# A hybrid decoder layer: the residual of the first token blocks added by engines, the third pair's weight parts ahead of spare sums, the last token block stored plainly

## The chip, the cores and the metric

The kernel runs on one core of a Trainium2 chip. Its engines work side by side and each takes its instructions in order: TensorE (PE in the profile, with PEld for its weight loads), VectorE (DVE), ScalarE (ACT), GpSimd (POOL) and SyncE (SP), which issues most transfers. The metric is the device time of one execution in microseconds (us), lower is better.

## The reference

One decoder layer on 1,024 tokens of width 1,024, in float32. What bears on this change is the frame around the two sub-layers, and the gated MLP:

```python
h = rms_norm(x, g_pre_mix[i]) * (1.0 + sc1) + sh1
...
x = x + gt1 * rms_norm(y @ w_out[i], g_post_mix[i])
h = rms_norm(x, g_pre_ffn[i]) * (1.0 + sc2) + sh2
x = x + gt2 * rms_norm(conv_ffn(h, w_up[i], ffn_conv_w[i], w_down[i]), g_post_ffn[i])
```

`conv_ffn` multiplies by `w_up` (1,024 x 5,632), runs a causal convolution of width 3 over tokens, applies `silu(a) * v` and multiplies by `w_down` (2,816 x 1,024). Between `h` and `y` stand a state-space mixer and a gated short convolution.

## The kernel before

Every product is made of three TensorE products: each factor is split into a high part (a cast on ACT) and a low part (a difference on VectorE or GpSimd), and the product of the two low parts is left out. The helper `mm3` (lines 475 to 479) issues them, and `tt` and `stt` (lines 867 and 870) are the two common VectorE operations, so these lines stand for many places; the tile names tell them apart.

**Order.** All work is written as generators ("threads"), and a planner, `Flow`, puts their steps in order before anything runs. A step names an engine and a cost (`D_` VectorE, `A_` ScalarE, `G_` GpSimd, `M_` TensorE, `L_` a transfer), or it waits for an event, for a free buffer of a ring (`get`), or for the landing of the thread's last transfer (`land`). The planner always takes the step that can start first, and among steps that can start within 0.02 us on that engine, the one with the lowest number in `PRIO`. It counts 2.1 us from the end of an issue to the landing. `SITES` says which engines may take an element-wise step; for `x2` that is VectorE alone. On the chip, each engine then runs its list in that order, waiting on semaphores; a step that waits holds all that stand behind it on its engine.

**The stage around the first residual.** The output projection (`t_out`) goes over three token blocks: block 0 of 512 tokens, blocks 1 and 2 of 256 each. A block has four tiles (`dp`), each with two groups of 128 channels. ACT scales a tile out of PSUM into `og` and squares it into `oq` (lines 1604 and 1606); the squares are summed, TensorE and some small steps make the norm of each token (`token_rstd`, lines 491 and 501), and then `t_resid` starts `t_x2` once for each tile: VectorE multiplies `og` by the norm, the input `x` is added, ACT squares the sum into `xr` (line 1713), SP stores it to `x2_dr`, and the squares are summed. `xr` is one of the four tables CL, Tr, Tz and St, left over from the mixer; `t_xr` hands them out, and CL keeps the sum of squares of its block until the second norm has been made. In blocks 0 and 1 the input is added by an accumulating transfer that POOL issues (line 1710), so `xr` is only a place for the squares. In block 2 `t_xr` loads the input into `xr` and VectorE adds it. After the second norm, `t_h2` makes the MLP's input, split into `h2h` and `h2l`.

**The up-projection** works on pairs of channel tiles (22 pairs). Pairs 0 and 1 are plain products (`t_ahead`, `t_first`): their parts on block 0, then those on block 1 and 2. From pair 2 on (`t_up`), a pair is a Strassen-Winograd product: seven products of 512 by 512, with the sums S1 to S4 of quarters of the MLP's input (`t_forms`, `t_forms2`) and sums of quarters of the weights. `t_pair_weights(i)` loads the two weight tiles of a pair, splits the first as it is (part a), makes differences, and splits them as part b, T2 and t; T2 and t lie in tiles named `wf` and `hm`. Pair 2 runs its products in the order 1 6 2 4 5 3 7: product 1 takes part a; 6 takes T2 and S2; 2 part a; 4 and 5 part t (5 with S1); 3 and 7 part b (with S4 and S3). The threads of the sums have the numbers 8.2 to 9.5, all of `t_pair_weights` 13. Behind the products come the convolution's taps on VectorE (`t_gate2`, number 2).

**The end.** The down-projection is another Strassen-Winograd product, seven products P1, P2, P5, P7, P6, P3 and P4 in this order, each over four token blocks of 128 (`tb`). `t_evict` and `t_half` put the eight blocks of the output together in halves of 512 columns, square and scale them; `t_final(b)` makes the norm of block `b`, has ACT scale each half by it (line 2364), and POOL add it to the output in memory by an accumulating transfer (line 2366). The output holds the transposed residual by then: `t_x2t` has put it there. The block made last is 7.

Of the kernel before, what the change touches and what calls it, by code (L numbers as in the profile page):

```python
# [16 lines left out]
ADD, SUB, MUL = ALU.add, ALU.subtract, ALU.mult  # L17

P = 128
# [5 lines left out]
H = 512  # L25
# [36 lines left out]
def _constants():  # L62
# [66 lines left out]
PRIO = {  # L129
    "t_small": 0,  # L130
    "t_loads": 6.0,
    "t_norm0": 7,
    "t_x": 1,
    "t_sh": 9,
    "t_h": 3.5,
    "t_u": 9.5,
    "t_bias": 0.5,
# [177 lines left out]
def hybrid_layer(ctx, tc, xT, w_adaT, w_ada0, w_u, w_bcv, w_out, w_up, w_down, glu_w, vec, ssm, con, out):  # L315
    nc = tc.nc
    outB = out.rearrange("(b p d) -> b p d", p=P, d=D)
    pe, dve, act, pool = nc.tensor, nc.vector, nc.scalar, nc.gpsimd
# [14 lines left out]
    fl = Flow({"k2": NK2, "k4": NK4, "hl": NHL, "raw": NRAW, "big": 3, "sm": 2, "nrm": 2, "s4": 0, "sn": 0, "wf0": 0, "wf1": 0, "hm0": 0, "hm1": 0, "cv": 0, "ca": 0, "gs": 0, "t5": 0, **{t: 1 for t in tables}})  # L333
# [3 lines left out]
    def nm(s):  # L337
        uid[0] += 1
        return f"{s}_{uid[0]}"
# [16 lines left out]
    def table(s, shape):  # L356
        return sp.tile([P] + shape, F32, tag=s, name=nm(s), bufs=1)

    def load(dst, src):
        nc.sync.dma_start(dst, src)  # L360


    def D_(n):
        return ("run", "dve", 0.07 + 1.04e-3 * n)

    def A_(n):
        return ("run", "act", 0.094 + 0.833e-3 * n)
# [7 lines left out]
    def L_(kb):  # L375
        return ("load", "dma", max(0.45, kb * 2.85e-3))

    def T_(site, o, a, b, op, n):

        e = yield ("pick", *({"dve": D_, "pool": G_}[e](n)[1:] for e in SITES[site]))  # L380
        {"dve": dve, "pool": pool}[e].tensor_tensor(o, a, b, op)  # L381
# [37 lines left out]
    def C(name, lo=0, hi=None):  # L419
        a, b = _CC[name]  # L420
        return ct[:, a + lo : (b if hi is None else a + hi)]
# [444 lines left out]
    def tt(o, a, b, op, eng=None):  # L866
        (eng or dve).tensor_tensor(o, a, b, op)  # L867

    def stt(o, a, s, b, op0, op1):
        dve.scalar_tensor_tensor(o, a, s, b, op0, op1)  # L870
# [654 lines left out]
    blocks = ((0, 0, H), (1, 0, H // 2), (1, H // 2, H))  # L1525
# [51 lines left out]
    def add_squares(site, bi, acc, q, i, n):  # L1577

        if i == 0:
            acc.append(q)  # L1580
        elif i == NT - 1 and bi == len(blocks) - 1 and SUM_ON_PE:
            acc.append(q)
        else:
            yield from T_(site, acc[0], acc[0], q, ADD, 2 * n)
# [92 lines left out]
    ev_xr = [[Event() for _ in range(NT)] for _ in blocks]  # L1677

    def t_xr():

        yield ("wait", ev_stat["a"])
        for bi, (hf, lo, hi) in enumerate(blocks):
            n = hi - lo
            for dp in range(NT):
                tag = ("CL", "Tr", "Tz", "St")[dp]
                yield ("get", tag)
                xr = table(tag, [1024])[:, : 2 * n]
                if bi == 2:
                    yield L_(n)
                    load(xr.rearrange("p (a t) -> p a t", a=2), x_of(bi, dp))  # L1690
                ev_xr[bi][dp].tile = xr, tag
                fl.fire(ev_xr[bi][dp], bi == 2)

    def x_of(bi, dp):
        hf, lo, hi = blocks[bi]
        return xT[2 * dp * P : (2 * dp + 2) * P, hf * H + lo : hf * H + hi].rearrange("(a p) t -> p a t", a=2)

    def t_x2(bi, dp, sl, n, og, r1, s2):

        two = "p (a t) -> p a t"  # L1700
        yield D_(2 * n)
        o3 = og.rearrange(two, a=2)
        tt(o3, o3, r1.unsqueeze(1).to_broadcast([P, 2, n]), MUL)
        yield ("wait", ev_xr[bi][dp])
        xr, tag = ev_xr[bi][dp].tile
        if bi == 2:
            yield from T_("x2", og, og, xr, ADD, 2 * n)
        else:
            yield ("load", "pool", 1.0)
            pool.dma_start(o3, x_of(bi, dp), accum_op=ADD)  # L1710
            yield ("land",)
        yield A_(2 * n)
        act.activation(xr, og, AF.Square)
        yield L_(n)
        load(x2_dr[2 * dp * P : (2 * dp + 2) * P, sl].rearrange("(a p) t -> p a t", a=2), o3)
        if dp:
            yield ("wait", s2[2][dp - 1])
        n_acc = len(s2[0])
        yield from add_squares(("sum_x2", "sum_x2", "sum_x2_last")[bi], bi, s2[0], xr, dp, n)
        if len(s2[0]) == n_acc:  # L1720
            fl.put(tag)
        else:
            s2[1].append(tag)
        fl.fire(s2[2][dp])
        if dp == NT - 1:
            fl.fire(ev_x2[bi], True)
# [73 lines left out]
    fl.spawn(t_out(), PRIO["t_out"])  # L1800
    fl.spawn(t_ahead(), PRIO["t_ahead"])
    fl.spawn(t_xr(), PRIO["t_xr"])


# [3 lines left out]
    def ptile(p, tag, shape, dt, bufs=1):  # L1808
        return pools[p].tile([P] + shape, dt, tag=tag, name=nm(tag), bufs=bufs)

    def E_(n, elsewhere=False):

        return ("run", "dve", 0.155 + 1.045e-3 * n)
# [65 lines left out]
    def hl_tile():  # L1879
        return hp.tile([P, 2, 1024], F32R, tag="hl", name=nm("hl"))  # L1880

    def odd_even(what, i):

        return ptile("ab"[i % 2], what, [2, 1024 if what == "hm" else H], F32R)

    def split(t, w, n, site="split_d"):

        yield A_(n)
        act.copy(t[:, 0, :n], w)  # L1889
        yield from TT_(site, t[:, 1, :n], w, t[:, 0, :n].bitcast(F32), SUB, n)  # L1890

    def TT_(site, o, a, b, op, n):
        if SITES[site] == ("dve",):
            yield from dve_tt(o, a, b, op, n)
        else:
            yield from T_(site, o, a, b, op, n)
# [5 lines left out]
    def t_pair_weights(i):  # L1902
        ev = pw[i]
        yield ("wait", pw[i - 1]["loaded"] if i > 2 else wev["up", NFF + 1][2])
        yield ("get", "raw", 2)
        wa, wb = (wp.tile([P, 1024], F32, tag="raw", name=nm("w")) for _ in range(2))
        yield L_(512)
        load(wa, w_up[i])
        yield L_(512)
        load(wb, w_up[NFF + i])  # L1910
        fl.fire(ev["loaded"])
        yield ("land",)
        yield ("wait", pw[i - 1]["t"] if i > 2 else wev["up", NFF + 1][0])
        yield ("get", "hl")
        ev["a"].tile = hl_tile()
        yield from split(ev["a"].tile, wa, 1024, "split_a")
        fl.fire(ev["a"])
        b11, b21, b12, b22 = wa[:, :H], wa[:, H:], wb[:, :H], wb[:, H:]

        yield from TT_("wsum" if i > 2 else "split_d", b11, b12, b11, SUB, H)  # L1920
        yield from TT_("wsum" if i > 2 else "split_d", b12, b22, b12, SUB, H)
        yield ("get", "hl")
        ev["b"].tile = hl_tile()
        yield from split(ev["b"].tile, wb, 1024)
        fl.fire(ev["b"])
        yield from TT_("wsum" if i > 2 else "split_d", b22, b22, b11, SUB, H)
        q = i % 2
        yield ("get", f"wf{q}")
        ev["T2"].tile = odd_even("wf", q)
        yield from split(ev["T2"].tile, b22, H)  # L1930
        fl.fire(ev["T2"])
        yield from TT_("wsum" if i > 2 else "split_d", b21, b21, b22, SUB, H)
        fl.put("raw")
        yield ("get", f"hm{q}")
        ev["t"].tile = odd_even("hm", q)
        yield from split(ev["t"].tile, wa, 1024)
        fl.put("raw")
        fl.fire(ev["t"])
# [108 lines left out]
    def cv(tag):  # L2047
        return ptile("ba"[tag == "ca"], tag, [T], F32, NCA if tag == "ca" else NCV)
# [61 lines left out]
    ev_x2t = Event()  # L2110
# [122 lines left out]
    NTB = NB // 2  # L2233
    LATE = 7
    banks = {}
    ev_prod = {(p, tb): Event() for p, _ in PRODUCTS for tb in range(NTB)}
# [113 lines left out]

    def t_final(b):

        for c in range(2):
            yield ("wait", ev_half[b, c])
        f = fin[:, b, :]
        yield D_(1)
        tt(f[:, 0:1], f[:, 0:1], f[:, 1:2], ADD)
        r = f[:, 1:2]
        yield from rsqrt(r, f[:, 0:1], 1.0 / D, (f[:, 2:3], f[:, 3:4]), EPS, 1, C("eps", 0, 1))
        yield ("wait", ev_x2t)  # L2360
        for c in range(2):
            u, of = half[b, c]
            yield A_(H + 100)
            act.activation(u, u, AF.Copy, scale=r)
            yield ("load", "pool", 1.0)
            pool.dma_start(outB[b, :, c * H : (c + 1) * H], u, accum_op=ADD)  # L2366
            if of:
                fl.spawn(t_put(of), 0)
        yield ("land",)

    def t_put(tag):
        yield ("land",)
        fl.put(tag)
# [20 lines left out]
        for dp in range(2):  # L2394
            fl.spawn(t_forms(s, dp), PRIO["forms"][s])
    for i in range(2, NFF):
        fl.spawn(t_pair_weights(i), PRIO["weights"])
    fl.spawn(t_x2t(), PRIO["t_x2t"])
    fl.spawn(t_all_up(), PRIO["t_ffn"])
    fl.spawn(t_gate2(), PRIO["t_gate2"])  # L2400
# [88 lines left out]
```

## Time and profile before

| What | us |
|---|---|
| Median of 3 runs | 1170.17 |
| Lowest and highest | 1169.62 and 1173.97 |
| The profiled execution | 1169.3 |
| Its span, first to last instruction | 1167.5 |

The profile is of one execution. The page gives each engine's busy time; the view of waits says which instruction waited for which; the view by stretch gives busy time within a part of the span, with the clock that TensorE was granted as a share of full speed; the order of time lists instructions with their start, their length, and in brackets the idle time before them with what ended it. A row such as `og<-og,CL` names the tiles written and read. Times of matmuls overlap, since they are pipelined. The rough order of the span: the mixer up to about 370 us, the output projection with the residual up to about 490 us, the pairs of the up-projection up to about 940 us, and the down-projection up to 1156 us.

### The profile page before, as it was taken

The page shows a single profiled execution, that of the slowest core. Times are in us where ns is not written, and L with a number is a line of the kernel's source. Part 1 is how long each engine was busy: PE and PEld are TensorE (multiplying, and loading weights), DVE is VectorE, ACT ScalarE, POOL GpSimd, SP SyncE. Part 2 cuts the span into 40 slices and gives each one's busy share as a digit, 9 for nine tenths or more (in the row PEclk, how much of TensorE's full clock was granted, in tenths as well). Part 3 has the DMA queues.
Part 4 walks back from the last instruction along what each step waited for, and adds up shares of the span by engine and source line. Part 5 has one row for each costly group of instructions (what it writes and reads, how often), then busy time and mean ns, then how long its engine had stood idle before and what let it go on. Part 6 is the DMA issues. An engine that isn't in the chain of part 4 may idle for free.

```text
span 1167.5 us, 13965 instructions
## 1 busy us (share of the span) xinstructions
PE 1056.0 (90%) x5012; PEld 855.6 (73%) x5012; DVE 877.8 (75%) x1212; ACT 486.7 (42%) x676; POOL 473.6 (41%) x475
## 2 busy tenths in 40 slices
PE   2987999999779956897999999999999999999995
PEld 2765778778446956785788888888888887888884
DVE  6769768897996335898778897889879978554752
ACT  4435322232344423555343333433433456454453
POOL 4799455652594022201444443434444320242013
PEclk9978989999899977799999999999999999999998
DMA  7533312337652274642532332233224498999338
GB/s 278 223 138 128 113 37 77 95 129 246 224 198 84 80 163 125 189 143 75 189 131 96 113 131 83 81 125 120 86 77 134 165 270 262 256 210 296 103 65 123
DMA packets 88533, 171.02 MB, mean 146 GB/s; under 512 B 8720, under 2 KB 34064, under 8 KB 88464
## 3 DMA queue, kind: packets, MB, share of 16 engines
q1 hardware_dynamic: 77648, 151.25, 37.9%
q0 software_dynamic: 10816, 18.88, 10.0%
q8 instruction: 39, 0.64, 0.2%
q14 instruction: 30, 0.25, 0.1%
HBM read 132.64 MB, written 37.46 MB: 146 GB/s over the span
## 4 chain that ended last, share of the span: by engine, by line
PE 44%; POOL 15%; issue 15%; DVE 12%; DMA 9%; ACT 3%; SPq 1%; POOLq 0%; DVEq 0%; ACTq 0%
PE big L475 9%; PE big L477 9%; PE big L479 9%; PE sm L475 5%; PE sm L479 5%; PE sm L477 5%; DMA wd<-in_w_down_dram 3%; POOL pa L381 2%; DMA w<-g_dr 2%; POOL Pt L381 1%; POOL wd L2217 1%; POOL out_dram L2366 1%; POOL pt L894 1%; POOL yl L381 1%; POOL pt L900 1%
## 5 line engine op out<-in xcount | busy, mean ns | idle before, releaser
L381 POOL TENSOR_TENSOR hl<-w,hl 128x1024 fp32r<-128x1024 f32 x34 | 86.8, 2554 | 253.6 <-ACT hl L1889 145.6
L381 POOL TENSOR_TENSOR w<-w,w 128x512 f32<-128x512 f32 x57 | 86.3, 1514 | 83.1 <-DVE hl L867 80.1
L1889 ACT CAST hl<-w 128x1024 fp32r<-128x1024 f32 (+1 forms) x65 | 66.5, 1023 | 49.4 <-issue 20.2
L2217 POOL DMA_DIRECT2D wd<-in_w_down_dram x44 | 38.3, 891 | 113.2 <-PE big L2266 29.4
L475 PE MATMUL big<-yh,hl 128*128 128x256 f32 (+1 forms) x192 | 67.7, 352 | 13.3 <-ACT hl L461 13.1
L867 DVE TENSOR_TENSOR wl<-wd,wh 128x512 fp32r<-128x512 f32 x77 | 51.0, 686 | 36.6 <-ACT wh L2221 36.6
L479 PE MATMUL big<-yh,hl 128*128 128x256 f32 (+1 forms) x192 | 65.9, 343 | 13.0 <-POOL hl L381 11.6
L477 PE MATMUL big<-yl,hl 128*128 128x256 f32 (+1 forms) x192 | 65.9, 343 | 7.6 <-POOL yl L381 7.6
L2221 ACT CAST wh<-wd 128x512 fp32r<-128x512 f32 x77 | 46.8, 620 | 54.8 <-DMA wd<-in_w_down_dram 53.5
L870 DVE SCALAR_TENSOR_TENSOR ca<-big,vec,ca 128x896 f32<-128x896 f32 (+1 forms) x92 | 65.1, 740 | 4.5 <-ACT ca L2055 4.5
L479 PE MATMUL big<-h,hl 128*128 128x512 f32 x192 | 60.8, 399 | 5.2 <-POOL hl L381 5.2
L475 PE MATMUL big<-h,hl 128*128 128x512 f32 x192 | 63.2, 411 | 0.8 <-DVE yb L867 0.4
L867 DVE TENSOR_TENSOR hl<-w,hl 128x1024 fp32r<-128x1024 f32 (+1 forms) x45 | 52.8, 1174 | 14.6 <-ACT hl L1889 14.6
L461 ACT CAST hl<-w 128x1024 fp32r<-128x1024 f32 x43 | 44.8, 1045 | 44.8 <-PE big L479 31.5
L475 PE MATMUL big<-s,hl 128*128 128x512 f32 x160 | 63.2, 395 | 0.0
L477 PE MATMUL big<-s,hl 128*128 128x512 f32 x160 | 63.1, 394 | 0.0
L479 PE MATMUL big<-s,hl 128*128 128x512 f32 x160 | 62.9, 393 | 0.0
L477 PE MATMUL big<-h,hl 128*128 128x512 f32 x192 | 61.3, 399 | 1.3 <-DVE h L725 1.3
L870 DVE SCALAR_TENSOR_TENSOR cv<-big,vec,cv 128x896 f32<-128x896 f32 (+1 forms) x84 | 58.3, 739 | 5.3 <-ACT cv L2055 5.3
L475 PE MATMUL big<-h2h,hl 128*128 128x512 f32 (+1 forms) x160 | 60.4, 378 | 0.0
L479 PE MATMUL big<-h2h,hl 128*128 128x512 f32 (+1 forms) x160 | 59.6, 373 | 0.7 <-DVE hl L381 0.7
L477 PE MATMUL big<-h2l,hl 128*128 128x512 f32 (+1 forms) x160 | 59.6, 373 | 0.0
(359 smaller groups left out, 3178.7 us busy)
## 6 DMA issues: line engine op xcount, KB each, us to landing
w<-in_w_up_dram SPq DMA_DIRECT2D x44, 512.0 KB, 4.0
w<-g_dr SPq DMA_DIRECT2D x35, 512.0 KB, 5.6
g_dr<-cv SPq DMA_DIRECT2D x53, 256.0 KB, 2.3
wd<-in_w_down_dram SPq DMA_DIRECT2D x44, 256.0 KB, 7.4
wd<-in_w_down_dram POOLq DMA_DIRECT2D x44, 256.0 KB, 6.5
w<-in_w_out_dram SPq DMA_DIRECT2D x20, 512.0 KB, 3.3
WBT<-in_w_adaT_dram SPq DMA_DIRECT2D x16, 512.0 KB, 3.7
w<-in_w_bcv_dram SPq DMA_DIRECT2D x13, 512.0 KB, 3.6
```

Source lines behind the costliest of these rows:

```text
L381: {"dve": dve, "pool": pool}[e].tensor_tensor(o, a, b, op)
L461: act.copy(t[:, 0, :], w)
L475: pe.matmul(outs[i], wh, xh[i], start=start, stop=False)
L477: pe.matmul(outs[i], wh, xl[i], start=False, stop=False)
L479: pe.matmul(outs[i], wl, xh[i], start=False, stop=stop)
L867: (eng or dve).tensor_tensor(o, a, b, op)
L870: dve.scalar_tensor_tensor(o, a, s, b, op0, op1)
L894: small_steps.append(lambda e: [lambda: e.tensor_tensor(o, a, b, op)])
L900: return [lambda: e.tensor_scalar(tT, a, s, None, op0), lambda: e.tensor_tensor(o, tT, b, op1)]
L1889: act.copy(t[:, 0, :n], w)
L2217: pool.dma_start(w, block_of(made[1], kk), accum_op=ADD)
L2221: act.copy(hi, w)
```

## The change

There are three parts. In the first, `t_xr` loads the input for all three blocks, and `t_x2` adds it in all three as it did in block 2 alone. The function `x_of` goes. In the second, the thread of pair 2's weights gets the number 8.9. In the third, `t_final` treats blocks 3 and 7 in another way: once P3 of token block 0 is done and the residual stands in the output, it takes a tile of the ring `cv` and loads the 128 rows into it; VectorE multiplies each half by the norm and adds the loaded residual in one operation, and SP stores the half.

```diff
                 xr = table(tag, [1024])[:, : 2 * n]
-                if bi == 2:
-                    yield L_(n)
-                    load(xr.rearrange("p (a t) -> p a t", a=2), x_of(bi, dp))
+                yield L_(n)
+                load(
+                    xr.rearrange("p (a t) -> p a t", a=2),
+                    xT[2 * dp * P : (2 * dp + 2) * P, hf * H + lo : hf * H + hi].rearrange("(a p) t -> p a t", a=2),
+                )
                 ev_xr[bi][dp].tile = xr, tag
-                fl.fire(ev_xr[bi][dp], bi == 2)
+                fl.fire(ev_xr[bi][dp], True)
...
         xr, tag = ev_xr[bi][dp].tile
-        if bi == 2:
-            yield from T_("x2", og, og, xr, ADD, 2 * n)
-        else:
-            yield ("load", "pool", 1.0)
-            pool.dma_start(o3, x_of(bi, dp), accum_op=ADD)
-            yield ("land",)
+        yield from T_("x2", og, og, xr, ADD, 2 * n)
...
     def t_final(b):
 
+        plain = b % NTB == NTB - 1
+        if plain:
+            yield ("wait", ev_prod["P3", 0])
+            yield ("wait", ev_x2t)
+            yield ("get", "cv")
+            x = cv("cv")
+            yield L_(512)
+            load(x, outB[b])
+            yield ("land",)
...
         for c in range(2):
             u, of = half[b, c]
+            if plain:
+                sl = slice(c * H, (c + 1) * H)
+                yield E_(H)
+                stt(x[:, sl], u, r, x[:, sl], MUL, ADD)
+                yield L_(256)
+                load(outB[b, :, sl], x[:, sl])
+                continue
             yield A_(H + 100)
             act.activation(u, u, AF.Copy, scale=r)
             yield ("load", "pool", 1.0)
...
     for i in range(2, NFF):
-        fl.spawn(t_pair_weights(i), PRIO["weights"])
+        fl.spawn(t_pair_weights(i), 8.9 if i == 2 else PRIO["weights"])
```

More of the change, by code (lines that the diff above doesn't have):

```diff
@@ L1687, in t_xr @@
                 xr = table(tag, [1024])[:, : 2 * n]
-                if bi == 2:
-                    yield L_(n)
-                    load(xr.rearrange("p (a t) -> p a t", a=2), x_of(bi, dp))
+                yield L_(n)
[3 more added lines that the diff above has]
+                )
                 ev_xr[bi][dp].tile = xr, tag
-                fl.fire(ev_xr[bi][dp], bi == 2)
-    def x_of(bi, dp):
-        hf, lo, hi = blocks[bi]
-        return xT[2 * dp * P : (2 * dp + 2) * P, hf * H + lo : hf * H + hi].rearrange("(a p) t -> p a t", a=2)
+                fl.fire(ev_xr[bi][dp], True)
     def t_x2(bi, dp, sl, n, og, r1, s2):
```

## The prediction

> **What bounds it now.** I read the page's busy table first, then who TensorE waited for, then busy time by stretch, then the order of time inside the worst stretch.
>
> ```profile
> span 1167.5 us, 13965 instructions
> PE 1056.0 (90%) x5012; PEld 855.6 (73%) x5012; DVE 877.8 (75%) x1212; ACT 486.7 (42%) x676; POOL 473.6 (41%) x475
> ```
>
> TensorE is the busiest engine by far, so what it loses in idle time, or at a low clock, is the time to win. The waits of PE in 410 to 560 us (total, times, longest) are the largest it has after the convolution:
>
> ```profile
> PE big L475 <- ACT hl L461: 13.1, 1, 13.1
> PE big L479 <- POOL hl L381: 11.6, 1, 11.6
> PE sm L475 <- ACT wf L1889: 6.7, 1, 6.7
> ```
>
> Busy time by stretch (length, then PE, PEld, DVE, ACT, POOL, granted clock, DMA share, GB/s):
>
> ```profile
> 410.00:560.00 150.00, 112.86 (x647) 101.00 (x646) 106.12 (x180) 71.48 (x128) 29.61 (x16) 0.82 0.51 144
> 480.00:560.00 80.00, 71.33 (x390) 60.55 (x389) 71.70 (x130) 45.45 (x86) 12.40 (x5) 0.93 0.44 147
> 560.00:600.00 40.00, 39.55 (x183) 32.15 (x183) 29.15 (x33) 16.47 (x20) 17.94 (x12) 1.00 0.45 151
> 431.00:451.00 20.00, 17.19 (x84) 16.72 (x85) 8.28 (x17) 6.95 (x13) 3.51 (x2) 0.59 0.53 143
> 470.00:482.00 12.00, 10.99 (x61) 10.79 (x62) 9.96 (x19) 6.51 (x10) 2.65 (x2) 0.66 0.51 146
> ```
>
> In 410 to 560 PE is idle 150 - 112.86 = 37.1 us, and after each long wait it works at a clock of 0.59 and 0.66: 17.19 x 0.41 + 10.99 x 0.34 = 10.8 us more. From 560 on (39.55 of 40 busy) it is nearly full until the end. So the 150 us around the residual are the place, and they are lost to this:
>
> ```profile
> 428.45 1.06 ACT L1713 ACTIVATE Tz<-og 128x1024 f32<-128x1024 f32 x1 [5.10 <-DMA og<-in_xT_dram]
> 429.42 0.46 ACT L1604 ACTIVATE og<-big,col 128x256 f32<-128x256 f32 x1
> 429.77 1.03 ACT L461 CAST hl<-w 128x1024 fp32r<-128x1024 f32 x1
> ```
>
> The square of the new residual stands on ACT until the accumulating transfer has landed; behind it in ACT's queue stands the cast of the next output weights, and PE stands until that cast is done (the 13.1 us above). The 11.6 us are the same thing one block later. The transfers (their tile's view):
>
> ```profile
> L1710 POOL DMA_DIRECT2D og<-in_xT_dram x8: 1204/1214/1398, 410.0 to 466.4; - x8
> DMA to landing us min/median/max: 4.2/5.3/8.0
> ```
>
> Each transfer is issued only after the square before it, so four latencies stand in a row in each block.
>
> **Edit 1: eight engine adds in place of eight accumulating transfers.** It removes the transfers above and about 8 x 1.21 = 9.7 us of POOL issue. It adds eight VectorE adds; the rows of their shapes, two inputs in SBUF, are (x, then total and mean ns):
>
> ```profile
> L381 DVE TENSOR_TENSOR CL<-CL,Tr 128x1024 f32<-128x1024 f32 x1 | 1.2, 1225 | 8.5 <-ACT Tr L1713 8.5
> L381 DVE TENSOR_TENSOR og<-og,CL 128x512 f32<-128x512 f32 x1 | 0.7, 685 | 0.0
> ```
>
> 4 x 1.225 + 4 x 0.685 = 7.6 us of DVE. The chain of a block gets shorter by far. Now, first multiply to last sum:
>
> ```profile
> 408.08 3.47 DVE L867 TENSOR_TENSOR og<-og,sm 128x1024 f32<-128x1024 f32 x3
> 437.90 1.23 DVE L381 TENSOR_TENSOR CL<-CL,St 128x1024 f32<-128x1024 f32 x1 [5.84 <-ACT St L1713]
> 451.06 2.48 DVE L867 TENSOR_TENSOR og<-og,sm 128x512 f32<-128x512 f32 x4 [1.37 <-PE sm L501]
> 473.09 0.68 DVE L381 TENSOR_TENSOR CL<-CL,St 128x512 f32<-128x512 f32 x1
> ```
>
> that is 31.1 and 22.7 us. After: four multiplies, four adds and three sums of 1.225 (13.5), one square (1.06) and handing over, some 15 us; in the second block 11 x 0.685 = 7.5, 0.63 and handing over, some 9. So the chains give 16 + 14 = 30 us, the clock 10.8 more, and PE's ceiling for the stage (all idle time and all slow clock) is 37.1 + 10.8 = 48.
>
> But DVE does not allow that. It has 106.12 us of work in these 150, and gets 7.6 more: 113.8. If it never stands, the stage takes 113.8 and the gain is **36.2**; at the share that it reached in its densest 80 us (71.70 of 80, 0.896) the stage takes 127.0 and the gain is **23.0**. I take the middle, 121 us, a gain of **29**: some of DVE's gaps in 480 to 560 are waits on the stalls that go, but new waits come, for the loads. What is late next is therefore VectorE, and the norm of the third block that waits for it.
>
> The loads: eight more on SP (four of 512 KB, four of 256 KB); the bytes are those of the transfers removed. For the first block they go out once the group statistics have freed the tables, among the first output weights, just ahead of this stretch:
>
> ```profile
> 360.39 1.05 ACT L461 CAST hl<-w 128x1024 fp32r<-128x1024 f32 x1 [5.11 <-PE big L479]
> 358.00:365.00 7.00, 7.00 (x29) 4.53 (x28) 5.34 (x9) 3.21 (x5) 2.71 (x2) 1.00 0.11 11
> ```
>
> There the DMA moves 11 GB/s and the next cast waits 5.1 us for a buffer that PE frees, not for its load: cost nothing; without that cover, up to the landing of one load, 6 us. For the second and third block the first table (CL) holds the sum of squares, and comes free only after the block before has had its norm; the other loads queue behind it. The third block's loads are in the kernel already:
>
> ```profile
> CL<-in_xT_dram SPq DMA_DIRECT2D x1, 256.0 KB, 5.0
> St<-in_xT_dram SPq DMA_DIRECT2D x1, 256.0 KB, 5.8
> ```
>
> Meanwhile DVE has the block before to scale and split,
>
> ```profile
> L870 DVE SCALAR_TENSOR_TENSOR og<-og,col,sm 128x512 f32<-128x512 f32 x8 | 5.7, 741 | 0.4 <-PE sm L501 0.4
> L870 DVE SCALAR_TENSOR_TENSOR h2l<-og,mod,h2h 128x512 fp32r<-128x512 f32 x8 | 5.7, 748 | 0.0
> ```
>
> 11.4 us for the first block, which covers 5.8; a wait there stands at the head of DVE's queue with everything behind it. Between 0 and 5.8 us a block; I take 3, within the 29.
>
> One row speaks against putting adds on DVE:
>
> ```profile
> 466.78 3.79 DVE L381 TENSOR_TENSOR CL<-CL,Tz 128x512 f32<-128x512 f32 x1 [3.15 <-ACT Tz L1713]
> 467.17 2.83 POOL L381 TENSOR_TENSOR hl<-w,hl 128x1024 fp32r<-128x1024 f32 x1
> ```
>
> Such a sum takes 0.69 alone; beside a POOL split it took 3.79, 3.1 more. (The Trainium skill, SBUF — State Buffer, section Who interferes with whom, has a rule for it: a VectorE instruction with two SBUF inputs and a GpSimd one that reads SBUF take one port pair as a whole, and the later one is blocked. By this rule each add next to a split can lose most of the split; the trace agrees, with the 3.79.) DVE's 106.12 holds the price for the old operations; for the new ones it is in the rivals.
>
> **Edit 2: weights of the third pair at 8.9 instead of 13.** The number of instructions stays, the order changes: four differences (0.68 by the rows below), two splits of 1,024 columns and one of 512 on DVE (1.225 and 0.685 by the rows of these shapes), casts on ACT, one split on POOL, the two weight loads on SP, all go ahead of the spare sums S1, S3, S4, behind the third block's h2. Now the difference chain stands 7 us between its first and second step, while DVE does sums and convolution:
>
> ```profile
> 539.76 0.68 DVE L867 TENSOR_TENSOR w<-w,w 128x512 f32<-128x512 f32 x1
> 546.74 0.68 DVE L867 TENSOR_TENSOR w<-w 128x512 f32<-128x512 f32 x1
> ```
>
> PE waits 6.7 us for the part wf at its end. With the gap closed that wait goes. Late next are the spare sums, pushed back by up to 4 x 0.68 + 3.1 = 5.8 us of DVE; PE has four products before the last ones, which cover it. Worth 0 to 6.7; it moves DVE work and removes none, so I don't add it to the 29: it lets the stage reach DVE's floor.
>
> **Edit 3: last block stored plainly.** Blocks 3 and 7 load their rows once the first P3 product is done (cover: the rest of P3 and P4 on PE; without it, one landing), use one VectorE operation a half, and store from SP. The end now:
>
> ```profile
> 1158.83 0.16 DVE L405 SCALAR_TENSOR_TENSOR fin<-fin 128x1 f32<-128x1 f32 x1
> 1159.65 0.70 ACT L2364 ACTIVATE wf<-wf,fin 128x512 f32<-128x512 f32 x1
> 1160.76 1.16 POOL L2366 DMA_DIRECT2D out_dram<-wf  x1
> ```
>
> From there to 1167.5 are 6.7 us. After: 1159.0 plus two operations of 0.7 is 1160.4, then issue and landing of a plain store of 256 KB:
>
> ```profile
> out_dram<-xt SPq DMA_DIRECT2D x16, 256.0 KB, 2.5
> x_dr<-og SPq DMA_DIRECT2D x8, 256.0 KB, 4.4
> ```
>
> 1160.4 + 2.5 = 1162.9, or 1164.8 with the busier row: a gain of 4.6 or 2.7. I take **4.5**.
>
> **Sum.** The profiled execution took 1169.3 us, 1.8 over its span and 0.9 under the median of the runs, 1170.17. 1169.3 - 29 - 4.5 = 1135.8, so **1136**.
>
> **Rivals.**
> - DVE's work slides: of 560 to 600 DVE is free 40 - 29.15 = 10.9 us, and what isn't urgent goes there. 1169.3 - 36.2 - 10.9 - 4.5 = **1118**. Against it: PE's wait for sums at the third pair.
> - VectorE is blocked: all eight adds meet a POOL split, 8 x 3.1 = 24.8; 1136 + 24.8 = 1161; with half of them, about **1150**. For it: POOL, freed of issues, may get more splits; against: POOL is busy in 29.61 of the 150 us only.
> - The change doesn't do what it says: the adds wait for their loads as the squares waited for transfers; only the tail is left, **1165**. Against: the first block's loads go out before 365 us, and its first multiply is at 408.08.
> - Slower: SP's queue. A residual load stands behind a weight load that waits for a ring slot:
>
> ```profile
> SPq L360 <- DVE hl L381: 46.7, 9, 12.8
> ```
>
> 12.8 us, plus 5.8 landing, with all of DVE behind the add: 18.6 in each of two blocks, 37.2 in all; 1136 + 37 = **1173**. It decides from about 17 us a block on. Against: the third block's load went out 21 us ahead of its use.
>
> ```profile
> 478.40 0.42 SPq L360 DMA_DIRECT2D CL<-in_xT_dram  x1
> 499.42 0.69 DVE L381 TENSOR_TENSOR og<-og,CL 128x512 f32<-128x512 f32 x1
> ```
>
>
> **How the numbers follow.** Forecast (23 to 36 in the stage, 2.7 to 5 in the tail: 1128 to 1144) 0.62; sliding 0.08; blocked or partly waiting (1144 to 1163) 0.17; tail only 0.05; SP's queue 0.08. The range takes the forecast whole, the nearer half of sliding and most of blocked: low is DVE's floor with half of the free time, 1169.3 - 36.2 - 5.5 - 4.5 = 1123; high is a stage gain of 10 with the smaller tail, 1169.3 - 10 - 2.7 = 1157. Half a per cent, about what a measurement of this kernel can tell, is 5.9 us: faster 0.62 + 0.08 + 0.17 = 0.87, same 0.05, slower 0.08.
>
> **What would show it.** Right: no wait of PE over 3 us from 396 us to the third pair, no clock of 0.59; DVE over 0.9 busy there; the third pair's wf no longer a wait; the last store landing some 4 us after its last VectorE operation. Wrong: adds on DVE with several us idle before them <-DMA (loads late); adds of 2 us and more beside POOL (port); a new wait for S1, S3 or S4 in the third pair (edit 2 paid back); PE waits after 560 for convolution results, which would mean that DVE's work only moved.

## The result and the profile after

The changed kernel takes 1138.77 us (median of 4 runs, 1135.78 to 1141.48); the kernel before took 1171.11 us in the runs beside it (1169.62 to 1173.97). The ratio is 0.972, with a 95% interval of 0.9687 to 0.9753. (Two executions that took 1738 and 3581 us, one of the kernel before and one of an experiment, are in no comparison below.) The profiled execution of the changed kernel took 1135.78 us, the shortest of the four, with a span of 1134.0 us instead of 1167.5, so 33.5 us less. The head of its page:

```profile
span 1134.0 us, 13972 instructions
PE 1049.4 (93%) x5012; PEld 848.6 (75%) x5012; DVE 889.3 (78%) x1218; ACT 482.9 (43%) x672; POOL 473.9 (42%) x469
```

PE has the same 5012 matmuls in a shorter span. VectorE's busy time rose from 877.8 to 889.3 us, and its instructions from 1212 to 1218. That is eight adds and four operations of the last blocks more, and six splits of weights less, which the change's description doesn't have and the prediction only as an argument for a rival: `SITES` lets VectorE or POOL take these splits, and the planner, with eight issues less for POOL and eight adds more for VectorE, gave six of them to POOL (70 of the 1,024-column splits `hl<-w,hl` on VectorE before and 64 after, 34 and 40 on POOL).

To see where the 33.5 us went, I cut both spans at instructions that both kernels have. The **stage**, as the word is used from here on, runs from the last evacuation of block 0's output projection on ACT to the first product with `wf` of pair 6 on PE (the expectations call it "the sixth pair"). In the order of time its two ends are, before:

```profile
396.40 1.27 ACT L1604 ACTIVATE og<-big,col 128x512 f32<-128x512 f32 x2 [7.81 <-PE big L479]
...
552.35 0.79 PE L475 MATMUL sm<-s,wf 128*128 128x512 f32 x1 [6.72 <-ACT wf L1889]
...
635.50 0.40 PE L475 MATMUL sm<-s,wf 128*128 128x512 f32 x1
```

and after:

```profile
393.96 1.27 ACT L1604 ACTIVATE og<-big,col 128x512 f32<-128x512 f32 x2 [7.81 <-PE big L479]
...
519.54 0.51 PE L475 MATMUL sm<-s,wf 128*128 128x512 f32 x1 [2.37 <-ACT xt L2125]
...
604.77 0.39 PE L475 MATMUL sm<-s,wf 128*128 128x512 f32 x1
```

The middle row is the same product of the third pair. Up to it the kernel before took 155.95 us and the changed one 125.58, so 30.4 less; up to the end of the stage 239.10 and 210.81, so 28.3 less. The rest of the 33.5: 2.4 us before the stage starts, where only the first block's four loads are new, 3.5 in the tail (from the last VectorE step of the last rsqrt to the end of the span), and between the stage's end and that step 0.7 us more.

Busy time in the stage (length, then PE, PEld, DVE, ACT, POOL, granted clock, DMA share, GB/s), before and then after:

```profile
396.40:635.50 239.10, 201.51 (x1101) 175.87 (x1100) 172.78 (x256) 108.34 (x173) 59.80 (x35) 0.89 0.46 140
```

```profile
393.96:604.77 210.81, 194.39 (x1101) 170.10 (x1099) 184.69 (x259) 108.15 (x173) 65.30 (x33) 0.96 0.46 149
```

It is the same work of PE (1101 matmuls). VectorE does 11.9 us *more* in 28.3 us *less*; PE's idle time in the stage goes from 37.6 to 16.4 us, and its granted clock from 0.89 to 0.96. The stretch of the prediction, and PE's waits in 396 to 545 us, in the changed kernel:

```profile
410.00:530.00 120.00, 105.98 (x638) 95.20 (x637) 111.49 (x175) 67.86 (x123) 36.86 (x16) 0.93 0.45 147
...
431.00:451.00 20.00, 18.99 (x133) 18.61 (x134) 17.63 (x31) 13.55 (x24) 8.90 (x4) 0.84 0.67 209
```

```profile
PE sm L491 <- issue: 5.6, 2, 4.8
PE sm L2123 <- DVE og L870: 2.6, 1, 2.6
PE sm L475 <- ACT xt L2125: 2.4, 1, 2.4
PE sm L501 <- DVE nrm L405: 2.3, 1, 2.3
```

In 431 to 451, where the clock had been 0.59, it is 0.84; it is low for a shorter time, 0.52 in the 7 us from 428 to 435. The waits of 13.1, 11.6 and 6.7 us are gone. The longest left, 4.8 us, is PE's wait to add up the squares of the first block's sum. The view names no releaser for it ("issue"), but VectorE's order shows one: the last fold of `CL` runs from 426.25 for 1.64 us, and PE starts at 427.99. VectorE is busy 111.49 of 120 us, 0.93.

The new adds in VectorE's order of time:

```profile
407.91 1.21 DVE L381 TENSOR_TENSOR og<-og,CL 128x1024 f32<-128x1024 f32 x1
409.09 2.84 DVE L381 TENSOR_TENSOR oq<-oq,oq 128x512 f32<-128x512 f32 x1
411.86 3.42 DVE L381 TENSOR_TENSOR og<-og,Tr 128x1024 f32<-128x1024 f32 x1
...
419.20 3.42 DVE L381 TENSOR_TENSOR CL<-CL,Tr 128x1024 f32<-128x1024 f32 x1
...
437.69 0.68 DVE L381 TENSOR_TENSOR og<-og,CL 128x512 f32<-128x512 f32 x1
...
438.89 2.89 DVE L381 TENSOR_TENSOR og<-og,Tz 128x512 f32<-128x512 f32 x1
```

No add has idle time before it, so no load is late. Six of the eight take the 1.21 or 0.68 us forecast, and two take 3.42 and 2.89, 2.2 us more each. POOL's splits lie at those moments:

```profile
408.21 5.99 POOL L381 TENSOR_TENSOR hl<-w,hl 128x1024 fp32r<-128x1024 f32 x2 [36.39 <-ACT hl L461]
418.65 2.89 POOL L381 TENSOR_TENSOR hl<-w,hl 128x1024 fp32r<-128x1024 f32 x1 [4.45 <-ACT hl L461]
...
438.63 2.60 POOL L381 TENSOR_TENSOR hl<-w,hl 128x1024 fp32r<-128x1024 f32 x1 [1.67 <-DVE og L381]
```

The six splits that went to POOL are all in the stage. VectorE's group of them there, before and then after:

```profile
L381 DVE TENSOR_TENSOR hl<-w,hl 128x1024 fp32r<-128x1024 f32 x10 | 12.2, 1222 | 3.6 <-ACT hl L461 3.5
```

```profile
L381 DVE TENSOR_TENSOR hl<-w,hl 128x1024 fp32r<-128x1024 f32 x4 | 4.9, 1221 | 3.5 <-ACT hl L461 3.5
```

### The profile page after: what moved, and what is told of

It reads as the page before. It is cut to its first block, busy times and chain, and to the rows that moved or that the text cites. A ratio compares the mean times of both kernels' runs of the same rounds, so it can differ in the third digit from the quotient of the medians.

```text
span 1134.0 us, 13972 instructions
## 1 busy us (share of the span) xinstructions
PE 1049.4 (93%) x5012; PEld 848.6 (75%) x5012; DVE 889.3 (78%) x1218; ACT 482.9 (43%) x672; POOL 473.9 (42%) x469
## 5 line engine op out<-in xcount | busy, mean ns | idle before, releaser
L381 POOL TENSOR_TENSOR hl<-w,hl 128x1024 fp32r<-128x1024 f32 x40 | 102.9, 2575 | 284.7 <-ACT hl L1882 149.0
L1882 ACT CAST hl<-w 128x1024 fp32r<-128x1024 f32 (+1 forms) x65 | 66.5, 1023 | 47.7 <-issue 22.9
L477 PE MATMUL big<-yl,hl 128*128 128x256 f32 (+1 forms) x192 | 63.4, 330 | 7.5 <-POOL yl L381 7.5
L867 DVE TENSOR_TENSOR hl<-w,hl 128x1024 fp32r<-128x1024 f32 (+1 forms) x45 | 52.9, 1174 | 16.4 <-ACT hl L1882 16.3
L475 PE MATMUL big<-yh,hl 128*128 128x256 f32 (+1 forms) x192 | 64.9, 338 | 0.1
L479 PE MATMUL big<-yh,hl 128*128 128x256 f32 (+1 forms) x192 | 63.3, 330 | 0.1
```

The costliest lines, as they stand in the source:

```text
L475: pe.matmul(outs[i], wh, xh[i], start=start, stop=False)
L477: pe.matmul(outs[i], wh, xl[i], start=False, stop=False)
L479: pe.matmul(outs[i], wl, xh[i], start=False, stop=stop)
```

## The experiments

The theory (A) is that the order of four latencies, standing in ACT's queue, was the stall, and that VectorE's work sets the stage once it is gone. Lengths of the stage are compared, because the time up to its start, in which the kernels differ only by the first block's four loads, varied by 8 us between profiles, with these loads and without them.

**Each edit alone.** Only the residual adds:

```diff
-        plain = b % NTB == NTB - 1
+        plain = False
...
-        fl.spawn(t_pair_weights(i), 8.9 if i == 2 else PRIO["weights"])
+        fl.spawn(t_pair_weights(i), PRIO["weights"])
```

> Only the residual of the first two blocks is changed (edit 1); the third pair's weights stand at 13 and the last blocks accumulate as before. Theory A (the four latencies in a row, which stood in ACT's queue, are the source; VectorE's work then sets the stage): 22 to 29 us below before, so about 1146, with no wait of PE over 3 us between 396 us and the end of the first pair; the wait for wf of the third pair (6.7 us before) is there again, 3 to 7 us. Rival B (the order of the weights is what lets VectorE fill its gaps): no more than 15 us below before, 1156 or more.

Measured: 1143.47 us beside 1169.43 of before, ratio 0.9793 (0.9755 to 0.9832). The stage takes 213.25 us. The wait for `wf` is there again, 4.4 us:

```profile
526.20 0.80 PE L475 MATMUL sm<-s,wf 128*128 128x512 f32 x1 [4.38 <-ACT wf L1882]
```

A holds, with one miss: the wait of 4.8 us for the first block's sum is there in this kernel too. The six splits on POOL come with this edit (VectorE has 64 here as well), so its worth includes them.

Only the third pair's weights, the kernel before with 8.9 at `i == 2`:

> Only the third pair's weight parts are moved (edit 2); the accumulating transfers stay. Theory A: the two stalls of PE of 13.1 and 11.6 us stay; the 6.7 us wait for wf goes; time 0 to 6.7 us below before, about 3. Rival B: 10 us and more below before, as the stage is then filled without edit 1.

Measured: 1168.33 us, ratio 0.9983 (0.9957 to 1.0009), which the times alone can't tell from no change. The stage takes 235.15 us, 4.0 less than before. PE's waits in 396 to 545 us begin as in the kernel before, and the one for `wf` is gone:

```profile
PE big L475 <- ACT hl L461: 13.4, 1, 13.4
PE big L479 <- POOL hl L381: 12.5, 1, 12.5
```

Only the last block stored plainly, the kernel before with the new `t_final`:

> Only blocks 3 and 7 are stored plainly (edit 3). From the start of the last VectorE step of the last rsqrt to the end of the span 5.2 us instead of 8.7, as in the changed kernel: 3.5 us below before. Rival: the tail's plain load of the rows early in the last stage takes SP's queue or VectorE's time that others need; then the gain is under 2 us.

Measured: 1166.57 us, ratio 0.9982 (0.9956 to 1.0007). The stage takes 239.24 us, the 239.10 of before again; from the last rsqrt step to the end are 5.48 us, 3.2 fewer than before. So the tail's gain is seen in the trace; it is too small for these times to tell.

Edits 1 and 3 without edit 2:

> Edits 1 and 3, without the move of the third pair's weights. If the parts are additive: the sum of the gains of residual only and tail only. Theory A: 1 to 6 us above the changed kernel, which had 1138.8: 1140 to 1145, with the wait for wf in the third pair again. Rival (edit 2 is worth nothing once edit 1 is in, since the spare sums are then late by as much): the same as the changed kernel within 1 us.

Measured: 1142.61 us, ratio 0.9776 (0.9735 to 0.9818), 3.8 above the changed kernel but with intervals that overlap. The stage takes 214.77 us, and the wait for `wf` is 4.2. With the two stages without edit 2 (213.25 and 214.77, mean 214.0) and those with it (212.1, below), edit 2 is worth 1.9 us on top of edit 1, and 4.0 alone. The 1.9 is less than the 2.2 us by which the three stages with it differ, so only the shorter wait is shown, not a gain. The tail's gain can't be seen in this kernel's time either: it is 0.9 us under that of edit 1 alone.

**How far the stage repeats.** The changed kernel again:

> The changed kernel once more, with a second profile, to say how far the stage's length repeats. If the lengths of the stage (block 0's last evacuation to the sixth pair) differ between profiles only by what the kernels do: 210.8 us again within 1 us, whatever the time before the stage is (that varied from 394 to 400 us). If the stage takes part in the run-to-run variation: 208 to 214, and differences of 2 to 4 us between the experiments say nothing.

Measured: 1138.46 us, ratio 0.9739 (0.9689 to 0.979). The stage takes 212.47 us, 1.7 more than in the first profile, and 213.04 in the run on the tail, which has the same stage. The mean of the three is 212.1, and their mean busy VectorE time is 184.9 us. The three lie 2.2 us apart, so differences of 2 us and less between stages are not read, and the 4.0 of edit 2 alone is near that limit. Against the two stages with the old one (239.10 and 239.24, mean 239.2), edit 1 alone is worth 239.2 - 214.0 = 25.2 us, and edits 1 and 2 are worth 27.1.

**More work on VectorE, early and late, and less.** The first block's h2l operations three times over:

```diff
         stt(b, og, mod[:, 3, k : k + 1], a.bitcast(F32), ADD, SUB)
+        for _ in range(2 if bi == 0 else 0):
+            stt(b, og, mod[:, 3, k : k + 1], a.bitcast(F32), ADD, SUB)
```

> The changed kernel with the eight h2l operations of the first block (128x512, 0.74 us each) carried out three times instead of once: 16 x 0.74 = 11.8 us more on VectorE, in an order that is otherwise the same; nothing waits for the repeats but VectorE's own queue. Theory A (VectorE's work sets the stage): VectorE had 120 - 111.5 = 8.5 us free in 410 to 530, so not all can hide; the stage (block 0's last evacuation to the sixth pair) gets 8 to 12 us longer, 1147 to 1151. Rival L (PE's own work and the latencies of the chains set it): no more than 4 us longer, under 1143.

Measured: 1156.53 us beside 1167.96 of before, ratio 0.9893 (0.9833 to 0.9953). The third block's, five times over (`range(4 if bi == 2 else 0)`):

> The changed kernel with the eight h2l operations of the third block (128x256, 0.40 us from start to start) carried out five times: 32 x 0.40 = 12.8 us more on VectorE, as many as the repeats in the first block, which made the stage 18.1 us longer, but at 483 to 490 us, where PE had its 20.0 us of 20 full and a clock of 1.00. If the sum of VectorE's work in the stage alone decides: 13 to 18 us longer again. If the place decides (PE has the products ahead and the first pairs to do there): under 8 us longer.

Measured: 1156.84 us beside 1166.87, ratio 0.9897 (0.9836 to 0.9959). Without the eight adds:

```diff
-        yield from T_("x2", og, og, xr, ADD, 2 * n)
+        if bi == 2:
+            yield from T_("x2", og, og, xr, ADD, 2 * n)
+        else:
+            yield D_(2 * n)
```

> The changed kernel without its eight new VectorE adds: the loads, squares and sums stay, and x isn't added in the first two blocks (that part of the computation is left out). 7.6 us of VectorE by the bare durations go, 14 us with the stalls of three of them next to a split on POOL. Theory A: the stage gets 6 to 10 us shorter, 1129 to 1133. Rival L: the adds lie beside PE's work; less than 3 us shorter.

Measured: 1131.47 us (the middle one of three) beside 1167.96, ratio 0.9697 (0.9629 to 0.9765). Their stages by busy time, in this order:

```profile
400.56:629.50 228.94, 201.06 (x1100) 175.66 (x1099) 199.81 (x275) 108.38 (x173) 64.75 (x33) 0.92 0.42 137
```

```profile
395.31:625.54 230.23, 199.52 (x1101) 173.05 (x1099) 200.73 (x291) 107.98 (x173) 65.79 (x33) 0.92 0.41 136
```

```profile
396.93:600.14 203.21, 190.52 (x1100) 166.37 (x1099) 174.67 (x251) 108.02 (x173) 63.51 (x33) 0.97 0.48 154
```

| Kernel | VectorE busy, against 184.9 | Stage, against 212.1 |
|---|---|---|
| h2l repeated in block 0 | +14.9 | +16.8 |
| h2l repeated in block 2 | +15.8 | +18.1 |
| no adds | -10.2 | -8.9 |

In these three kernels the stage follows VectorE's busy time nearly one to one, in both directions and from both places. That refutes the rival L, which allowed 4 us at most. It doesn't tell VectorE's sum of work from the length of the chain through it: each repeat writes the tile of h2l that PE reads, and the adds stand in the chain to the second norm, so they lengthen both. The sum alone doesn't set the stage, as the next two kernels show. My 8 to 12 us for the first were too few, for two reasons that the table shows: VectorE was busy 14.9 us longer, not 11.8 (the h2l of 512 columns took 0.91 us in the mean, not 0.74), and the 8.5 us of free time on VectorE took none of them up. So the free time of this queue was no room; that it is the time in which VectorE waits for what its neighbours make of its own results is how I read the order of time, and wasn't tried by itself. The repeats in block 2 show that a full PE (20.0 of 20 us busy, clock 1.00, in 471 to 491) is no cover for VectorE either; PE ran out a little later, with four waits for `h2l` of 10.2 us in all, between 496 and 511 us. These are tiles that the repeats write, so it isn't so that nothing waits for the repeats but VectorE's own queue.

**Whether POOL's splits take VectorE's time.** All splits of the output and first up weights on VectorE:

```diff
-                yield from T_("split", t[:, 1, :], w, t[:, 0, :].bitcast(F32), SUB, 1024)
+                yield from T_("split_d" if key[0] in ("o", "up") else "split", t[:, 1, :], w, t[:, 0, :].bitcast(F32), SUB, 1024)
...
-        yield from split(ev["a"].tile, wa, 1024, "split_a")
+        yield from split(ev["a"].tile, wa, 1024, "split_a" if i > 2 else "split_d")
```

> The changed kernel with all splits of the output and first up weights, and the first split of the third pair, on VectorE (1.21 us each); POOL did 13 of them between 408 and 506 us. Rival P, port (a split on POOL blocks VectorE for about 2.2 us, as the adds of 3.42 beside 1.21 and the sum of 2.84 beside 0.68 show): 12 or 13 more splits cost VectorE about 15 us and give back the some 17 us that its operations stood; the stage is the same within 4 us. If POOL's splits are free to VectorE: 12 to 15 us longer, 1151 and more.

Measured: 1142.58 us, ratio 0.979 (0.9743 to 0.9838). The stage takes 218.31 us, 6.2 more, which neither theory had. Its busy time, and the groups of 395 to 530 us with their shapes (total us, mean ns):

```profile
394.44:612.75 218.31, 194.45 (x1101) 170.34 (x1099) 176.49 (x270) 108.53 (x173) 35.02 (x21) 0.94 0.44 144
```

```profile
L381 DVE TENSOR_TENSOR hl<-w,hl 128x1024 fp32r<-128x1024 f32 x15 | 18.2, 1221 | 5.6 <-ACT hl L461 5.6
L381 DVE TENSOR_TENSOR oq<-oq,oq 128x512 f32<-128x512 f32 x5 | 3.5, 691 | 0.1
L867 DVE TENSOR_TENSOR hl<-w,hl 128x1024 fp32r<-128x1024 f32 x2 | 2.4, 1218 | 1.5 <-ACT hl L1882 1.5
...
L381 DVE TENSOR_TENSOR og<-og,Tr 128x1024 f32<-128x1024 f32 x1 | 1.2, 1217 | 0.0
```

The same groups in the changed kernel:

```profile
L381 DVE TENSOR_TENSOR oq<-oq,oq 128x512 f32<-128x512 f32 x5 | 6.8, 1355 | 0.0
L381 DVE TENSOR_TENSOR hl<-w,hl 128x1024 fp32r<-128x1024 f32 x4 | 4.9, 1221 | 3.5 <-ACT hl L461 3.5
...
L381 DVE TENSOR_TENSOR og<-og,Tr 128x1024 f32<-128x1024 f32 x1 | 3.4, 3415 | 0.0
```

The price is shown: with the neighbour on POOL gone, the same sums take 691 ns in place of 1355, and the add 1217 in place of 3415. VectorE makes 17 splits in place of 5 (12 x 1.21 = 14.5 us more work), and is busy 176.5 us in place of 184.9. By this difference 184.9 - (176.5 - 14.5) = 22.9 us of its busy time in the changed kernel is standing beside these splits on POOL, 1.9 us for each of the 12 moved. (By the rule of the Trainium skill, SBUF — State Buffer, section Who interferes with whom, a VectorE instruction with two SBUF inputs contends with a GpSimd one that reads SBUF; the 3.42 beside 1.21 agree.) But the time didn't follow: with 8.4 us less on VectorE the stage is 6.2 us longer, because of the order. PE's waits in 396 to 660 us:

```profile
PE big L479 <- DVE hl L381: 16.8, 4, 7.9
```

Splits on VectorE stand behind the residual's operations, and PE waits for them. So the last kernel put them ahead:

```diff
-            fl.spawn(one_tile(), PRIO["weights"])
+            fl.spawn(one_tile(), 3.9 if key[0] in ("o", "up") else PRIO["weights"])
```

> The changed kernel with all splits of the output and first up weights on VectorE, as in the splits-on-VectorE run, but with their threads at 3.9, ahead of the residual's operations (4) and of h2 (8), so that each split stands in VectorE's queue as soon as its cast is there; the third pair's first split stays on POOL. With all splits on VectorE the stage took 218.3 us, 6 more than in the changed kernel (mean of three profiles 212.1), though VectorE was busy 8.4 us less: PE had waited 16.8 us for splits that stood late in VectorE's queue. If those waits were the price of the late order and the port's price is what is saved: PE's waits for splits fall under 5 us, the stage takes 200 to 208 us, 1130 to 1135. If the wait only moves (the norm's chain now stands behind the splits): 210 to 218, no gain over the changed kernel.

Measured: 1141.57 us, ratio 0.9749 (0.9693 to 0.9806); the stage takes 210.52 us, with VectorE busy 179.4. That is the second theory, no gain over the changed kernel. PE's waits for splits are gone, as the first theory had it, and the place to which the wait moved is telling. Up to the third pair's product it took 112.10 us, 14.8 less than the mean of the changed kernel's three profiles (125.58, 128.04, 127.12), and then gave that back behind ACT:

```profile
400.24:512.34 112.10, 106.15 (x721) 96.13 (x719) 102.32 (x166) 67.04 (x112) 8.68 (x4) 0.98 0.44 147
...
512.34:546.47 34.13, 22.85 (x94) 18.05 (x92) 24.23 (x44) 14.71 (x30) 14.05 (x6) 0.80 0.37 125
```

```profile
518.37 7.42 POOL L381 TENSOR_TENSOR hl<-w,hl 128x1024 fp32r<-128x1024 f32 x1 [21.54 <-ACT hl L1882]
```

```profile
528.50 1.04 ACT L1882 CAST hl<-w 128x1024 fp32r<-128x1024 f32 x1 [6.04 <-POOL w L381]
529.46 0.70 ACT L1833 CAST s<-og 128x256 fp32r<-128x256 f32 x2
530.07 0.58 ACT L2018 COPY sn<-sm 128x512 f32<-128x512 f32 x1
```

A cast of the fourth pair's weights waits for a difference on POOL; behind it in ACT's queue stands the copy that empties a PSUM tile, and PE waits 9.9 us for that tile. The difference was late because the split before it on POOL took 7.42 us (the next one, at 545.09, took 2.41): VectorE ran operations with two inputs in SBUF without a gap up to 523.60, and the split ended 2.2 us after that. By these rows it was POOL that stood here, beside VectorE. It is the stall of the kernel before once more, with another step in it. An order that keeps the first part's gain wasn't tried.

**The adds on POOL** ("x2" of blocks 0 and 1 at a site with `("pool",)`):

> The changed kernel with the eight adds of the first two blocks on POOL (about 2.4 us for 1,024 columns and 1.4 for 512 by its rows), put into POOL's order by the planner. Bare work (VectorE's instructions alone count): 7.6 us less on VectorE, 3 to 8 us faster than the changed kernel. Port theory: each POOL add blocks a VectorE operation for up to its own length, and the chain of a block gets 4 x 1.2 or 4 x 0.7 us longer; not faster, 0 to 10 us slower.

Measured: 1140.71 us, ratio 0.9775 (0.9733 to 0.9818); the stage takes 211.41 us, 0.7 less than the mean. This doesn't tell the theories apart as meant: with POOL taken, the planner gave VectorE 11 splits in place of 5, 6 x 1.21 = 7.3 us, about the 7.6 that the adds had cost. It only says that the exchange is worth nothing.

**The tail.** Blocks 6 and 7 stored plainly (`plain = b >= NB - 2`):

> The changed kernel with blocks 6 and 7 stored plainly, in place of 3 and 7: so no accumulating transfer is under way in the last 20 us but those of block 5 and earlier. If the last store's landing is held up by block 6's two accumulating transfers (issued at 1125.4 and 1126.0): the stretch from the last rsqrt step to the end is 4.7 us and less, in place of 5.2. If it is issue and landing of the last store alone: 5.2 again within 0.2.

Measured, in one run: 4.85 us from the last rsqrt step to the end, where the changed kernel's two profiles had 5.17 and 5.11. That is 0.3 less, between the two theories. The last store landed 2.0 us after the start of its issue, in place of 2.3, so block 6's transfers may cost it 0.3 us; one run doesn't show more. The rest is the two operations, 1.6 us, the store, and 1.2 us from its landing to the end of the span.

## Why the prediction was right, and where it wasn't

The forecast was 1136 us, the median 1138.77. Its sum for the profiled run was 29 + 4.5 = 33.5 us, and the span is shorter by 33.5; that this fits to the tenth is luck, as the tail was 1.0 too high and 2.4 us came from before the stage. Inside the stage, too, two things that the sum didn't have nearly cancelled: six splits that left VectorE, and operations that stood beside POOL.

- **The stalls.** Right in mechanism: with the transfers gone, so are the waits of 13.1 and 11.6 us, and the clocks of 0.59 and 0.66 (five pieces of 20 us from 431 on have 0.84 and more; the low clock that is left, 0.52, is in the 7 us behind the one long wait, 428 to 435). Edit 1 alone brought them about. "No wait of PE over 3 us" was wrong by one, the 4.8 us for the first block's sum. The first block's chain was forecast at some 15 us and takes 20.6 (405.64 to 426.2), as operations of 2.84, 3.42 and 3.42 us stand in it; the second takes 10.8 (435.29 to 446.1) for 9.
- **VectorE is late next.** Right, and the runs with more and less work on it show it, as far as the added work stands in the chain to h2. Where the order of its queue changed, the order decided and not the sum. The forecast put 113.8 us of work into 121; the same stretch, placed by its ends, takes 119.6 and 122.1 us in two profiles:

```profile
407.56:527.19 119.63, 105.61 (x644) 95.33 (x643) 111.12 (x172) 70.13 (x126) 38.19 (x16) 0.93 0.46 151
```

```profile
406.00:528.09 122.09, 106.82 (x643) 95.79 (x642) 111.90 (x172) 69.99 (x126) 38.10 (x16) 0.92 0.45 148
```

  The middle between VectorE's floor and its densest share was a choice, and it came out at a share of 0.93 and 0.92. About 2 us were given back in the four pairs after it (30.4 at the third pair, 28.3 at pair 6).
- **The adds' price.** The 7.6 us were too low: the eight adds took 12.0 us, the 7.6 and 2 x 2.2 for the two that met a split. Over the stage VectorE is busier by 184.9 - 172.8 = 12.1 us, but that this is the adds' 12.0 is chance: the six splits that went to POOL took 7.3 us off, and other operations, the same in number but for one, last 7.4 us longer on balance (the sums `oq<-oq,oq` alone 3.4). So the rival "VectorE is blocked" was at work beyond the two adds: its ground "POOL, freed of issues, may get more splits" came true, and its sign, adds of 2 us and more, showed twice. The 113.8 us of work were near the 111.1 and 111.9 measured in part because these terms nearly cancel. The prediction's row of 3.79 us shows the lengthening, but not that the later one stands: that sum starts at 466.78, before the split at 467.17.
- **The loads** cost nothing, as forecast for the first block, and nothing too for the second, where 3 was taken: issued at 429.91 to 431.44, used from 437.69 without a wait. Nothing of the rival with SP's queue showed.
- **Edit 2** was forecast at 0 to 6.7 and not added; it is worth 4.0 alone, and on top of edit 1 1.9, which is not told from nothing. The wait for `wf` became one of 2.4 us for `xt`. New waits for S1, S3 or S4 are not in the list.
- **The tail** was mis-sized: 3.5 us in place of 4.5 (from 8.67 to 5.17 us after the last rsqrt step). The step was "1160.4 + 2.5": it let the span end with the landing. From the last operation's end, 1130.43, to the end of the span are 3.57 us, of which the last store takes 2.3 from the start of its issue to its landing, near the 2.5 (order of time, then the store in its tile's view):

```profile
1129.69 0.74 DVE L870 SCALAR_TENSOR_TENSOR cv<-wf,fin,cv 128x512 f32<-128x512 f32 x1
```

```profile
L360 SPq DMA_DIRECT2D out_dram<-cv x1: 333/333/333, 1130.5 to 1130.5; - x1
DMA to landing us min/median/max: 2.3/2.3/2.3
```

  So it landed at 1132.8, and the span ended 1.2 us later, at 1134.0. In the kernel before the last transfer had landed at 1165.9, 1.6 us before the end.
- **Before the stage** 2.4 us came off. Of the change only the first block's four loads lie there. The start of the stage lay between 392.4 and 400.6 us in the profiles with them (392.40 in the second of the changed kernel, 400.56 with the first repeats) and between 394.8 and 398.1 in the three without, so this is run-to-run variation, and the shortest run happened to be profiled.

## What to carry to other kernels

Look in an in-order queue for the instruction that waits for a transfer or a slow engine, and price it by what stands behind it: here squares that waited 4.3 to 5.5 us, four in a row, and 2.3 to 3.9 us in the next block, cost PE two waits of 13.1 and 11.6 us and the slow clock after them. Before calling an engine's idle time room, add work to it and see where it stands in the chain: 15 us more on a VectorE that was free for 8.5 of 120 us cost 17 to 18. And count an instruction shared out to POOL with what it takes from VectorE: a split cost 1.9 us there, where VectorE makes it in 1.21. Where a planner shares steps out, count again after a change what each engine was given: here six splits moved that nobody had asked to move.

## What the runs showed of the hardware

The size of the price beside POOL: 22.9 us of VectorE's 184.9 in the stage, more than the eight adds. It can fall on POOL as well, with the split of 7.42 us in place of 2.41. And the slow clock after a wait: behind PE's 4.75 us of idle time at 423 to 428, its matmuls of 256 columns take 0.41 us and more until about 434.7, in place of 0.28 (the granted clock is 0.52 from 428 to 435), so the short wait costs some more after its end.

```profile
422.96 0.28 PE L479 MATMUL big<-yh,hl 128*128 128x256 f32 x1
427.99 1.84 PE L491 MATMUL sm<-con,CL 128*128 128x1 f32 x8 [4.75 <-issue]
...
434.32 0.41 PE L475 MATMUL big<-yh,hl 128*128 128x256 f32 x1
434.53 0.38 PE L477 MATMUL big<-yl,hl 128*128 128x256 f32 x1
434.74 0.29 PE L479 MATMUL big<-yh,hl 128*128 128x256 f32 x1
```
